# A two-block transformer kernel: compressed scores per projection in fp32, and scan products issued half a pair later with 17 factor buffers

## The chip, the cores and the metric

One core of one Trainium2 chip runs the whole program. The metric is the device time of one execution in microseconds (us).

## What is computed

Two blocks act on a sequence of 256 tokens of width 2048. The first is a sparse-attention block with a spatial gating branch. The second has an even layer (a bidirectional state-space scan next to a wide convolution) and an odd layer (neighbourhood attention). Two small parts matter here. In the first block each query is scored against 15 compressed keys:

```python
sc = jnp.einsum('bqgrd,bngd->bgrqn', qb, kc).astype(jnp.float32) * scale
sc = jnp.where(vc_mask, sc - slopes[:, :, None, None] * dc.astype(jnp.float32), NEG)
p_c = jax.nn.softmax(sc, axis=-1) * vc_mask
```

In the even layer the scan is, for each head and direction, a product of a decay matrix and a score matrix with the inputs:

```python
seg = A_cs[:, :, :, None] - A_cs[:, :, None, :]
Lmat = jnp.exp(jnp.where(tri, seg, -jnp.inf))
CB = jnp.einsum("bclgn,bcsgn->bclsg", Cc, Bc)
Y_diag = jnp.einsum("bclgsr,bcsgrp->bclgrp", CB[..., None] * Lmat, X)
```

## The kernel before

Nearly all work is projections. A weight piece of 128x1024 fp32 (`raw`) comes in by SP's DMA queue. ACT rounds it to `wh` (L98), DVE makes the rest `wl` (L99), and PE multiplies each of the eight 128x128 chunks three times (`mm3`, L120 to L122: high by high, high by low, low by high). A projection of the layers below is two such pieces, 48 matmuls. `raw`, `wh` and `wl` have four buffers each, so a new `wl` can only be written when PE is through with the piece four before. The output of a projection is a PSUM tile `acc`; while `K.wide` is set there are four of them.

The program is written as one stream, and a scheduler fixes the order of each engine's queue beforehand; each engine then runs its queue strictly in that order and waits at semaphores.

**Compressed scores (first block).** The compressed keys are split into a high and a low part, `kcbd[0]` and `kcbd[1]`. Eight query projections (`pj(0.125)`, evacuated by DVE at L321) are split into `qh` and `ql`. After all eight, 16 `mm3` of 32 columns each write the scores `scps`, and DVE starts the softmax (`sc`, L447).

**Scan (even layer).** There are 16 pairs of heads. For each pair, `ssd` makes nine factors `m`: `decay` takes a row of running sums from DRAM (`csb`, `cs0`), ACT does a Relu (L905) and an Exp (L906), and DVE multiplies by the scores (L907). The tag `m` has NM = 8 buffers. PE multiplies the first factor (L943) and then the other eight (L959) into `yps`, and DVE adds it to `yb` (L961). The pairs are spread over two runs of projections: 16 of `xs` (`conv5`: DVE makes four taps each, L876, on `cacc`; after each the transposes `xtp`), and then 16 of z (`za`: ACT Tanh L994, DVE L995). Behind z pair c is needed for `yb` times `za` (L1004). The sum of squares of all 16 closes the stage (`yss`, L210). After these come 16 projections `zb` (ACT Silu, L1043). Silu, and Exp with Tanh, are in different tables of ACT, so going from one to the other costs an ACT_TABLE_LOAD. All through these stages DVE also does the 480 taps of the wide convolution (`vb`, L845), metered out per weight piece.

**After `zb`.** The mean over `vb` (`lns`, `mean`, `lnm`) is taken, `yb` is split to `ah` and `al` (L164) for the output projection, and `vb` is centred (L1023).

Of the kernel before, what the change touches and what calls it, by code (L numbers as in the profile page):

```python
# [19 lines left out]
P = 128  # L20
# [15 lines left out]
NM, NK1 = 8, 6  # L36
# [217 lines left out]
def block1(K, a):  # L254
# [4 lines left out]
    with ExitStack() as ctx:  # L259
# [126 lines left out]
        kcbd = [wk.tile([P, 2, 2, 16], F32R, tag="kcbd%d" % i, bufs=1, name="kcbd%d" % i) for i in range(2)]  # L386
        for i in range(2):
            nc.vector.memset(kcbd[i].bitcast(F32), 0.0)
# [19 lines left out]
        for g in range(2):  # L408
            gs = slice(64 * g, 64 * g + 64)
            K.split(kcbd[0][gs, :, g, 0:15], kcbd[1][gs, :, g, 0:15],  # L410
                    cps[gs, :32].rearrange("q (p n) -> q p n", p=2)[:, :, 0:15])
            for p in range(2):
                nc.vector.tensor_copy(hidbd[gs, p, :, g, 0:15], hs[gs, 1, p, None, 0:15].to_broadcast([64, 4, 15]))
# [19 lines left out]
        qh, ql = t8("h0", F32R, "qh"), t8("h1", F32R, "ql")  # L433
        for j in range(8):
            K.split(qh[:, j, :], ql[:, j, :], pj(0.125))
# [3 lines left out]
        scps = K.ps.tile([P, 2, S], F32, tag="t", bufs=2, name="scps")  # L439
        for t in range(2):  # L440
            ts = slice(128 * t, 128 * t + 128)
            for j in range(8):
                p = j // 4
                K.mm3(scps[:, t, 32 * j : 32 * j + 32].rearrange("q (g n) -> q g n", g=2), qh[:, j, ts], ql[:, j, ts],
                      kcbd[0][:, p], kcbd[1][:, p], True, True)
# [235 lines left out]
def layer_e(K, a):  # L681
# [3 lines left out]
    with ExitStack() as ctx:  # L685
# [88 lines left out]

        def steps():
# [16 lines left out]
            yield 1.0  # L792
            nc.scalar.activation(ea[:64], par(K, "A_log")[:64], AF.Exp)
# [9 lines left out]
            for k, src in enumerate((dt, cs)):  # L803
                tp = K.ps.tile([P, 512], F32, tag="t", bufs=2, name="dtp")
                for i, (s0, s1) in enumerate(TT2[1:]):
                    nc.tensor.transpose(tp[:, 64 * i : 64 * i + 64], src[:, s0:s1], K.ident[:64, :64])
                for q in range(4):
                    r0 = 32 * (q // 2) + q % 2
                    nc.tensor.matmul(tp[32 * q : 32 * q + 32, 128:144], src[:, 0:32], K.ident[:64, r0 : r0 + 31 : 2],
                                     start=True, stop=True, skip_group_check=True)  # L810
                nc.scalar.activation(dtT[:, k].rearrange("p i r -> p (i r)"), tp[:, 0:128], AF.Copy)
                nc.scalar.activation(dt0[:, k], tp[:, 128:144], AF.Copy)
# [97 lines left out]
        def ssd(g):  # L910
# [19 lines left out]
            for i in (2 * g, 2 * g + 1):  # L930
                cs0 = wk.tile([P, T2], F32, tag="cs0", name="cs0")
                csbs = []
                for hh in range(2):
                    off = csd.offset + (2 * i + hh) * T2
                    csb = wk.tile([P, 2, T2], F32, tag="csb", bufs=3, name="csb")
                    nc.sync.dma_start(csb, bass.AP(tensor=csd.tensor, offset=off, ap=[[0, P], [32 * T2, 2], [1, T2]]))
                    csbs.append(csb)
                    for d in range(2):
                        q = 32 * (2 * d + hh)
                        nc.sync.dma_start(cs0[q : q + 32, :], bass.AP(tensor=csd.tensor, offset=off + 32 * d * T2, ap=[[0, 32], [1, T2]]))  # L940
                m0 = decay(cs0, dt0[:, 1, i : i + 1], dt0[:, 0, i : i + 1], cb0)
                yps = K.ps.tile([P, 512], F32, tag="o", bufs=1, name="yps")[:, :T2]
                nc.tensor.matmul(yps, xt[:, i, 0, :], m0, start=True, stop=False, skip_group_check=True)  # L943

                prods = []
                for d in range(2):
                    for ti in (1, 2):
                        s0, s1 = TT2[ti]
                        lo, hi = (s0, T2) if d == 0 else (0, s1)
                        for hh in range(2):  # L950
                            row = 32 * d + 2 * i + hh
                            m = decay(csbs[hh][:, d, lo:hi], dtT[:, 1, ti - 1, row : row + 1], dtT[:, 0, ti - 1, row : row + 1], C[d][ti])
                            prods.append((yps[64 * hh : 64 * hh + 64, lo:hi], xt[:, i, ti, 64 * hh : 64 * hh + 64], m))
                    if d:

                        prev = None
                        for k, (o, w, m) in enumerate(prods[::-1]):
                            with tc.issue_after(prev) if prev else nullcontext():
                                prev = nc.tensor.matmul(o, w, m, start=False, stop=k >= 6, skip_group_check=True).ins  # L959
                    yield 1.0  # L960
                nc.vector.tensor_tensor(yb[:, i, :], yb[:, i, :], yps, op=ALU.add)  # L961
                done[0] = i + 1
# [3 lines left out]
        def pump_ssd(n, upto=0):  # L966
            while ssdq and (n > 0 or done[0] < upto):
                try:
                    n -= next(ssdq[0])
                except StopIteration:  # L970
                    ssdq.pop(0)

# [422 lines left out]
```

## Time and profile before

| | us |
|---|---|
| median of 3 runs | 2270.6 (2270.43 to 2271.83) |
| the profiled execution | 2271.78 |
| its span, first to last instruction | 2269.9 |
| PE busy | 2218.4 (98%) |
| DVE busy | 1639.2 (72%) |
| ACT busy | 1162.1 (51%) |

The profiled execution is 1.2 us above the median, and 1.9 us of it lie outside the span. PE is busy for all but some 50 us, so the table says where to look: at the places where PE stands still, and at those where its clock is below full.

### The profile page before, as it was taken

Reading aid. Unit: us, or ns where it says so; the run is one execution under the profiler, and the core shown is the slowest. Engines: PE = TensorE matmul, PEld = TensorE weight load, DVE = VectorE, ACT = ScalarE, POOL = GpSimd, SP = SyncE. Lnnn points to the kernel's source line nnn. Section 1 sums busy time; section 2 is a strip of 40 time slices with the busy share of each in tenths; the row PEclk is TensorE's granted clock in tenths of the full one; section 3 lists DMA queues with packets and bytes.
Section 4 is the critical chain, followed back from the end, with each engine's and each line's share of the span. In section 5 each row is a group of like instructions: output and inputs, shape, how many; then the busy total and the mean of one; then the engine's idle time right before and its main releaser. Section 6 shows DMA issues by size and latency. Waiting matters only on the chain.

```text
span 2269.9 us, 44011 instructions
## 1 busy us (share of the span) xinstructions
PE 2218.4 (98%) x17702; PEld 2156.0 (95%) x17702; DVE 1639.2 (72%) x2891; ACT 1162.1 (51%) x2039; POOL 121.3 (5%) x114
## 2 busy tenths in 40 slices
PE   8999999999999999999998998899999999999997
PEld 7998799999999998999998998899999999999997
DVE  6557777555555669999999888798776666666654
ACT  4446654444444444454557887645444545444453
POOL 0000000000000230000000010002011000000011
PEclk9999999999999999999999999999999999999999
DMA  7642455555556554564454556354655555545453
GB/s 279 217 148 94 138 190 184 187 184 187 186 195 209 186 171 148 199 220 174 174 177 151 175 176 181 123 177 151 202 176 189 172 172 173 171 166 171 160 172 121
DMA packets 126412, 398.71 MB, mean 176 GB/s; under 512 B 16832, under 2 KB 33664, under 8 KB 125696
## 3 DMA queue, kind: packets, MB, share of 16 engines
q1 hardware_dynamic: 126064, 395.89, 51.6%
q8 instruction: 139, 2.28, 0.4%
q14 instruction: 65, 0.53, 0.1%
q10 hardware_dynamic: 144, 0.01, 0.0%
HBM read 391.45 MB, written 4.40 MB: 174 GB/s over the span
## 4 chain that ended last, share of the span: by engine, by line
PE 93%; DVE 3%; ACT 2%; DMA 1%; issue 1%; POOL 0%; SPq 0%; DVEq 0%; ACTq 0%; POOLq 0%
PE acc L120 28%; PE acc L122 28%; PE acc L121 28%; PE acc L156 1%; DVE wl L99 1%; DMA rawf<-in_w_in_fm 1%; PE yps L959 1%; DVE vb L845 1%; ACT wh L98 1%; PE o_ps L1210 1%; PE pt_ps L506 0%; PE sp L120 0%; PE sp L122 0%; PE sp L121 0%; PE o_ps L1208 0%
## 5 line engine op out<-in xcount | busy, mean ns | idle before, releaser
L98 ACT ACTIVATE wh<-raw 128x1024 fp32r<-128x1024 f32 x674 | 713.1, 1059 | 955.1 <-PE acc L121 580.1
L99 DVE TENSOR_TENSOR wl<-raw,wh 128x1024 fp32r<-128x1024 f32 x674 | 828.1, 1230 | 404.4 <-ACT wh L98 399.4
L120 PE MATMUL acc<-uh,wh 128*128 128x272 f32 (+1 forms) x1488 | 436.3, 293 | 15.7 <-DVE za L995 8.2
L121 PE MATMUL acc<-ul,wh 128*128 128x272 f32 (+1 forms) x1488 | 434.3, 292 | 0.0
L122 PE MATMUL acc<-uh,wl 128*128 128x272 f32 (+1 forms) x1488 | 434.3, 292 | 0.0
L120 PE MATMUL acc<-xh,wh 128*128 128x256 f32 (+1 forms) x1136 | 322.3, 284 | 0.0
L121 PE MATMUL acc<-xl,wh 128*128 128x256 f32 (+1 forms) x1136 | 322.3, 284 | 0.0
L122 PE MATMUL acc<-xh,wl 128*128 128x256 f32 (+1 forms) x1136 | 321.1, 283 | 0.1
L120 PEld LDWEIGHTS acc<-uh,wh 128*128 128x128 f32 (+1 forms) x1488 | 280.8, 189 | 19.5 <-DVE za L995 8.9
L122 PE MATMUL acc<-ouh,wl 128*128 128x256 f32 (+1 forms) x1024 | 296.6, 290 | 0.0
L121 PE MATMUL acc<-oul,wh 128*128 128x256 f32 (+1 forms) x1024 | 294.6, 288 | 0.0
L120 PE MATMUL acc<-ouh,wh 128*128 128x256 f32 (+1 forms) x1024 | 293.8, 287 | 0.0
L121 PEld LDWEIGHTS acc<-ul,wh 128*128 128x128 f32 (+1 forms) x1488 | 280.6, 189 | 3.5 <-issue 2.3
L122 PEld LDWEIGHTS acc<-uh,wl 128*128 128x128 f32 (+1 forms) x1488 | 280.2, 188 | 3.2 <-issue 2.3
L120 PEld LDWEIGHTS acc<-xh,wh 128*128 128x128 f32 (+1 forms) x1136 | 213.8, 188 | 1.4 <-DVE pj L319 0.4
L122 PEld LDWEIGHTS acc<-xh,wl 128*128 128x128 f32 (+1 forms) x1136 | 214.4, 189 | 0.4 <-DVE wl L99 0.3
L121 PEld LDWEIGHTS acc<-xl,wh 128*128 128x128 f32 (+1 forms) x1136 | 213.6, 188 | 0.5 <-issue 0.2
L122 PEld LDWEIGHTS acc<-ouh,wl 128*128 128x128 f32 x1024 | 192.5, 188 | 2.6 <-issue 2.6
L120 PEld LDWEIGHTS acc<-ouh,wh 128*128 128x128 f32 x1024 | 192.9, 188 | 0.0
L121 PEld LDWEIGHTS acc<-oul,wh 128*128 128x128 f32 x1024 | 192.7, 188 | 0.0
L845 DVE SCALAR_TENSOR_TENSOR vb<-early,par,vb 128x257 f32<-128x257 f32 (+9 forms) x330 | 150.3, 500 | 1.1 <-ACT vb L829 0.7
L204 POOL TENSOR_TENSOR sq<-sq 128x272 f32<-128x272 f32 (+1 forms) x44 | 50.6, 1150 | 741.0 <-issue 450.3
(417 smaller groups left out, 4295.7 us busy)
## 6 DMA issues: line engine op xcount, KB each, us to landing
raw<-in_e_w_in SPq DMA_DIRECT2D x184, 512.0 KB, 3.6
raw<-in_w_in_fm SPq DMA_DIRECT2D x140, 512.0 KB, 3.6
raw<-in_o_w_in SPq DMA_DIRECT2D x128, 512.0 KB, 3.9
raw<-in_e_w_out SPq DMA_DIRECT2D x64, 512.0 KB, 4.5
raw<-in_w_up SPq DMA_DIRECT2D x32, 512.0 KB, 3.6
raw<-in_w_out SPq DMA_DIRECT2D x32, 512.0 KB, 4.4
raw<-in_w_pg SPq DMA_DIRECT2D x32, 512.0 KB, 4.2
raw<-in_o_w_out SPq DMA_DIRECT2D x32, 512.0 KB, 4.4
```

The source lines that it names most:

```text
L98: nc.scalar.activation(wh, raw, AF.Copy)
L99: ins = nc.vector.tensor_tensor(wl, raw, wh.bitcast(F32), op=ALU.subtract)
L120: mm(out, lh, rh, start=start, stop=False)
L121: mm(out, lh, rl, start=False, stop=False)
L122: mm(out, ll, rh, start=False, stop=stop)
L156: self.nc.tensor.matmul(a, raws[c // 8][:, c % 8, :], x(c), start=c == 0, stop=c == 15)
L204: self.nc.gpsimd.tensor_tensor(acc, acc, sq, op=ALU.add)
L845: ins = nc.vector.scalar_tensor_tensor(v[:, lo:hi], u[:, lo + o : hi + o], par(K, "e_dw_w", 31 * b + k), v[:, lo:hi], op0=ALU.mult, op1=AL ...
L959: prev = nc.tensor.matmul(o, w, m, start=False, stop=k >= 6, skip_group_check=True).ins
L1210: nc.tensor.matmul(o_ps[64 * g : 64 * g + 64, ts], vt[:, 2 * t, 64 * g : 64 * g + 64], pt[:, g, :], start=False, stop=True, skip_group_che ...
```

## The change

There are four edits. The compressed keys stay in fp32 (one `kcbd`, written by ACT), and the scores of a query projection are two fp32 matmuls, issued right after that projection. The products of a scan pair are gathered in `finish` and issued after the first five factors of the next pair (or when the stage needs them), all nine in one run. The factors have 17 buffers; the memory for it comes from a smaller scratch area for dynamic DMA. Last, the transposes of `dt` come out before those of `cs` (`turned`).

```diff
-NM, NK1 = 8, 6
+NM, NK1 = 17, 6
...
-        kcbd = [wk.tile([P, 2, 2, 16], F32R, tag="kcbd%d" % i, bufs=1, name="kcbd%d" % i) for i in range(2)]
-        for i in range(2):
-            nc.vector.memset(kcbd[i].bitcast(F32), 0.0)
+        kcbd = wk.tile([P, 2, 2, 16], F32, tag="kcbd", bufs=1, name="kcbd")
+        nc.vector.memset(kcbd, 0.0)
...
-            K.split(kcbd[0][gs, :, g, 0:15], kcbd[1][gs, :, g, 0:15],
-                    cps[gs, :32].rearrange("q (p n) -> q p n", p=2)[:, :, 0:15])
+            nc.scalar.activation(kcbd[gs, :, g, 0:15], cps[gs, :32].rearrange("q (p n) -> q p n", p=2)[:, :, 0:15], AF.Copy)
...
+        scps = K.ps.tile([P, 2, S], F32, tag="t", bufs=2, name="scps")
         for j in range(8):
-            K.split(qh[:, j, :], ql[:, j, :], pj(0.125))
+            q = pj(0.125)
+            K.split(qh[:, j, :], ql[:, j, :], q)
+            for t in range(2):
+                nc.tensor.matmul(scps[:, t, 32 * j : 32 * j + 32].rearrange("q (g n) -> q g n", g=2),
+                                 q[:, 128 * t : 128 * t + 128], kcbd[:, j // 4], start=True, stop=True)
...
-        for t in range(2):
-            ts = slice(128 * t, 128 * t + 128)
-            for j in range(8):
-                p = j // 4
-                K.mm3(scps[:, t, 32 * j : 32 * j + 32].rearrange("q (g n) -> q g n", g=2), qh[:, j, ts], ql[:, j, ts],
-                      kcbd[0][:, p], kcbd[1][:, p], True, True)
...
-                m0 = decay(cs0, dt0[:, 1, i : i + 1], dt0[:, 0, i : i + 1], cb0)
-                yps = K.ps.tile([P, 512], F32, tag="o", bufs=1, name="yps")[:, :T2]
-                nc.tensor.matmul(yps, xt[:, i, 0, :], m0, start=True, stop=False, skip_group_check=True)
-
-                prods = []
+                prods = [decay(cs0, dt0[:, 1, i : i + 1], dt0[:, 0, i : i + 1], cb0)]
...
-                            prods.append((yps[64 * hh : 64 * hh + 64, lo:hi], xt[:, i, ti, 64 * hh : 64 * hh + 64], m))
-                    if d:
-
-                        prev = None
-                        for k, (o, w, m) in enumerate(prods[::-1]):
-                            with tc.issue_after(prev) if prev else nullcontext():
-                                prev = nc.tensor.matmul(o, w, m, start=False, stop=k >= 6, skip_group_check=True).ins
+                            prods.append((lo, hi, ti, hh, m))
+                    if d == 0:
+
+                        finish()
                     yield 1.0
-                nc.vector.tensor_tensor(yb[:, i, :], yb[:, i, :], yps, op=ALU.add)
-                done[0] = i + 1
+                ready.append((i, prods))
+
+        ready = []
+
+        def finish():
+
+
+            if not ready:
+                return
+            i, prods = ready.pop(0)
+            yps = K.ps.tile([P, 512], F32, tag="o", bufs=1, name="yps")[:, :T2]
+            prev = nc.tensor.matmul(yps, xt[:, i, 0, :], prods[0], start=True, stop=False, skip_group_check=True).ins
+            for k, (lo, hi, ti, hh, m) in enumerate(prods[:0:-1]):
+                with tc.issue_after(prev):
+                    prev = nc.tensor.matmul(yps[64 * hh : 64 * hh + 64, lo:hi], xt[:, i, ti, 64 * hh : 64 * hh + 64], m, start=False,
+                                            stop=k >= 6, skip_group_check=True).ins
+            nc.vector.tensor_tensor(yb[:, i, :], yb[:, i, :], yps, op=ALU.add)
+            done[0] = i + 1
...
+            if done[0] < upto:
+                finish()
...
-    nc = bacc.Bacc("TRN2", target_bir_lowering=False, num_devices=1)
+    nc = bacc.Bacc("TRN2", target_bir_lowering=False, num_devices=1, dynamic_dma_scratch_size=4096)
```

The scheduler's order of the two programs is the same on PE, ACT and DVE for most of the program. Three of the places that differ are shown here.

PE at the compressed scores, before: the 48 matmuls come in one run (31 of them, 22 of a projection in between, then the rest).

```order
L120 MATMUL acc<-xh,wh 128x256
L121 MATMUL acc<-xl,wh 128x256
L122 MATMUL acc<-xh,wl 128x256
L120 MATMUL scps<-kcbd_598,qh 128x32
L121 MATMUL scps<-kcbd_599,qh 128x32
L122 MATMUL scps<-kcbd_598,ql 128x32
L120 MATMUL scps<-kcbd_598,qh 128x32
L121 MATMUL scps<-kcbd_599,qh 128x32
```

The same engine after the change, at the first of the eight places:

```order
L120 MATMUL acc<-xh,wh 128x256
L121 MATMUL acc<-xl,wh 128x256
L122 MATMUL acc<-xh,wl 128x256
L438 MATMUL scps<-kcbd,pj 128x32 x2
L120 MATMUL acc<-xh,wh 128x256
L121 MATMUL acc<-xl,wh 128x256
```

Two fp32 matmuls now stand at eight places, 48 projection matmuls apart, half a projection behind the one whose queries they read.

ACT near the end of the scan, before: Silu of the first `zb` projections stands among the Exp of the last pairs, with a table load each way.

```order
L906 ACTIVATE m<-m 128x144
L1043 ACT_TABLE_LOAD
L1043 ACTIVATE zb<-acc 128x272
L906 ACT_TABLE_LOAD
L906 ACTIVATE m<-m 128x144
L201 ACTIVATE sq<-yb 128x272
L994 ACTIVATE zt<-acc 128x272
L905 ACTIVATE m<-csb,dtT 128x272
```

ACT at the same first `zb`, after (L908 is the Exp, L1007 the Tanh, L1056 the Silu):

```order
L908 ACTIVATE m<-m 128x272
L98 ACTIVATE wh<-raw 128x1024
L201 ACTIVATE sq<-yb 128x272
L1007 ACTIVATE zt<-acc 128x272
L98 ACTIVATE wh<-raw 128x1024
L201 ACTIVATE sq<-yb 128x272
L1007 ACTIVATE zt<-acc 128x272
L98 ACTIVATE wh<-raw 128x1024
L201 ACTIVATE sq<-yb 128x272
L98 ACTIVATE wh<-raw 128x1024
L1056 ACT_TABLE_LOAD
L1056 ACTIVATE zb<-acc 128x272
```

All factors and all z projections are now done before the first Silu; ACT's queue holds 5 table loads in place of 13.

DVE behind the mean over `vb`, before: `al` (L164) and the centring of `vb` (L1023) alternate, and the next weight piece comes after both.

```order
L1017 TENSOR_SCALAR mean<-lns 128x3
L218 TENSOR_SCALAR diag<-ident,mean 128x128 x2
L99 TENSOR_TENSOR wl<-raw,wh 128x1024
L164 TENSOR_TENSOR al<-yb,ah 128x272
L218 TENSOR_SCALAR diag<-ident,mean 128x128
L164 TENSOR_TENSOR al<-yb,ah 128x272 x7
L1023 TENSOR_TENSOR vb<-vb,lnm 128x272 x3
L164 TENSOR_TENSOR al<-yb,ah 128x272
L1023 TENSOR_TENSOR vb<-vb,lnm 128x272 x3
L164 TENSOR_TENSOR al<-yb,ah 128x272
L1023 TENSOR_TENSOR vb<-vb,lnm 128x272 x3
L164 TENSOR_TENSOR al<-yb,ah 128x272 x6
```

DVE at the same mean, after (L1030 the mean, L1036 the centring):

```order
L1030 TENSOR_SCALAR mean<-lns 128x3
L164 TENSOR_TENSOR al<-yb,ah 128x272 x3
L218 TENSOR_SCALAR diag<-ident,mean 128x128 x2
L164 TENSOR_TENSOR al<-yb,ah 128x272 x13
L218 TENSOR_SCALAR diag<-ident,mean 128x128
L99 TENSOR_TENSOR wl<-raw,wh 128x1024
L1073 TENSOR_TENSOR h_18187<-acc,hr 128x16
L1075 TENSOR_TENSOR h_18187<-acc,hr 128x4x32 x2
L1036 TENSOR_TENSOR vb<-vb,lnm 128x272 x12
```

All 16 `al` now stand together, and the weight piece comes before the centring.

## Rows read from the trace of the kernel before

**Rows 1.** The page: busy time and share of each engine.
```profile
PE 2218.4 (98%) x17702; PEld 2156.0 (95%) x17702; DVE 1639.2 (72%) x2891; ACT 1162.1 (51%) x2039; POOL 121.3 (5%) x114
```
**Rows 2.** Windows: stretch, width, then busy us of PE, PEld, DVE, ACT, POOL; PE clock, DMA.
```profile
1200.00:1250.00 50.00, 42.29 (x337) 40.22 (x336) 46.96 (x99) 40.06 (x103) 1.61 (x2) 1.00 0.47 151
1400.00:1450.00 50.00, 37.95 (x270) 34.22 (x269) 37.26 (x78) 36.34 (x79) 5.25 (x5) 0.90 0.38 118
```
**Rows 3.** Waits of PE from 1190 to 1470: us in total, times, longest.
```profile
PE acc L120 <- DVE za L995: 8.2, 2, 6.3
PE yps L959 <- DVE m L907: 5.0, 2, 3.2
PE acc L120 <- DVE cacc L876: 4.7, 3, 2.0
PE acc L120 <- ACT zb L1043: 2.8, 1, 2.8
PE yps L943 <- DVE m L907: 1.0, 2, 0.6
PE yss L210 <- POOL sq L204: 0.8, 1, 0.8
```
**Rows 4.** Windows around the compressed scores, columns as in rows 2.
```profile
144.00:148.00 4.00, 4.00 (x24) 4.00 (x23) 0.00 (x0) 0.00 (x0) 0.00 (x0) 0.57 0.37 131
148.00:152.00 4.00, 4.00 (x34) 4.00 (x34) 1.29 (x2) 1.06 (x1) 0.00 (x0) 0.91 0.01 4
152.00:156.00 4.00, 4.00 (x25) 4.00 (x25) 2.35 (x5) 0.70 (x1) 0.00 (x0) 0.66 0.33 123
```
**Rows 5.** Timeline of PE at scores and single fp32 matmuls: start us, us, instruction.
```profile
83.25 0.28 PE L120 MATMUL acc<-xh,wh 128*128 128x256 f32 x1
83.37 0.30 PE L407 MATMUL cps<-chs,w 128*128 128x32 f32 x2
...
83.71 0.28 PE L122 MATMUL acc<-xh,wl 128*128 128x256 f32 x1
...
148.03 0.26 PE L122 MATMUL scps<-kcbd,ql 128*128 128x32 f32 x1
...
150.37 0.26 PE L122 MATMUL scps<-kcbd,ql 128*128 128x32 f32 x1
...
1466.60 0.83 PE L210 MATMUL yss<-ones,sq 128*128 128x1 f32 x6 [0.76 <-POOL sq L204]
```
**Rows 6.** Timeline of ACT in the scan, with idle time before and its releaser.
```profile
1218.25 0.52 ACT L905 ACTIVATE m<-cs,dt 128x272 f32<-128x272 f32 x1 [2.59 <-PE yps L959]
...
1416.39 1.28 ACT L1043 ACT_TABLE_LOAD   x1
...
1418.10 1.28 ACT L906 ACT_TABLE_LOAD   x1
```
**Rows 7.** Windows of 6 us at the slow clock and at the mean, columns as in rows 2.
```profile
1422.00:1428.00 6.00, 6.00 (x43) 5.29 (x43) 1.67 (x3) 2.35 (x5) 0.00 (x0) 0.80 0.14 41
...
1434.00:1440.00 6.00, 5.68 (x33) 5.69 (x34) 2.65 (x7) 3.96 (x7) 0.81 (x1) 0.72 0.27 90
...
1542.00:1548.00 6.00, 3.32 (x16) 3.10 (x15) 6.00 (x14) 3.68 (x8) 4.03 (x5) 0.66 0.35 107
1548.00:1554.00 6.00, 6.00 (x40) 6.00 (x39) 4.17 (x6) 1.94 (x4) 4.54 (x3) 0.77 0.84 265
```
**Rows 8.** Waits of PE over the whole span, the three at the mean.
```profile
PE acc L122 <- DVE wl L99: 2.7, 1, 2.7
...
PE lnm L219 <- DVE diag L218: 0.7, 1, 0.7
PE acc L121 <- DVE al L164: 0.7, 1, 0.7
```
**Rows 9.** Waits of SP's queue from 1190 to 1470, and a landing time.
```profile
SPq L936 <- ACT m L905: 32.1, 12, 4.3
...
raw<-in_e_w_in SPq DMA_DIRECT2D x184, 512.0 KB, 3.6
```

More of the change, by code (lines that the diff above doesn't have):

```diff
@@ L433, in block1 @@
         qh, ql = t8("h0", F32R, "qh"), t8("h1", F32R, "ql")
+        scps = K.ps.tile([P, 2, S], F32, tag="t", bufs=2, name="scps")
         for j in range(8):
-            K.split(qh[:, j, :], ql[:, j, :], pj(0.125))
-        ptc = wk.tile([P, 2, S], F32, tag="ptc", bufs=1, name="ptc")
-        scps = K.ps.tile([P, 2, S], F32, tag="t", bufs=2, name="scps")
-        for t in range(2):
-            ts = slice(128 * t, 128 * t + 128)
-            for j in range(8):
-                p = j // 4
-                K.mm3(scps[:, t, 32 * j : 32 * j + 32].rearrange("q (g n) -> q g n", g=2), qh[:, j, ts], ql[:, j, ts],
-                      kcbd[0][:, p], kcbd[1][:, p], True, True)
+            q = pj(0.125)
[3 more added lines that the diff above has]
+                                 q[:, 128 * t : 128 * t + 128], kcbd[:, j // 4], start=True, stop=True)
+        ptc = wk.tile([P, 2, S], F32, tag="ptc", bufs=1, name="ptc")
         sc = wk.tile([P, 2, 16, 16], F32, tag="sc", bufs=1, name="sc")
@@ L773, in layer_e, with turned @@
         dt0 = wk.tile([P, 2, 16], F32, tag="dt0", bufs=1, name="dt0")
+        def turned(k, src):
+            tp = K.ps.tile([P, 512], F32, tag="t", bufs=2, name="dtp")
+            for i, (s0, s1) in enumerate(TT2[1:]):
+                nc.tensor.transpose(tp[:, 64 * i : 64 * i + 64], src[:, s0:s1], K.ident[:64, :64])
+            for q in range(4):
+                r0 = 32 * (q // 2) + q % 2
+                nc.tensor.matmul(tp[32 * q : 32 * q + 32, 128:144], src[:, 0:32], K.ident[:64, r0 : r0 + 31 : 2],
+                                 start=True, stop=True, skip_group_check=True)
+            nc.scalar.activation(dtT[:, k].rearrange("p i r -> p (i r)"), tp[:, 0:128], AF.Copy)
+            nc.scalar.activation(dt0[:, k], tp[:, 128:144], AF.Copy)
         def steps():
@@ L792, in steps @@
             yield 1.0
+            turned(0, dt)
+            yield 1.0
             nc.scalar.activation(ea[:64], par(K, "A_log")[:64], AF.Exp)
@@ L802, in steps @@
             nc.sync.dma_start(csd, cs)
[L803 to L812, printed above, removed]
+            turned(1, cs)
             yield 1.0
```

## The prediction, made before the changed kernel had run

> **What bounds the kernel now.** I read the page first. PE is busy for 98% of the span [rows 1], so a change can only gain where PE stands still, where its clock is below full, or where it is given less to do. The windows of 50 us come next, to find such places. The reader is to see that in 1200 to 1250 PE has 42.29 us of work in 50 while DVE has 46.96, and that in 1400 to 1450 nobody is full: PE 37.95, DVE 37.26, ACT 36.34 [rows 2]. The first place is short of DVE time. The second is a chain in which the engines take turns.
>
> The waits of PE name these chains. From 1190 to 1470, which is the scan, PE waits 22.5 us in six groups [rows 3]: 5.0 and 1.0 for a factor `m`, 4.7 for the taps of `conv5`, 8.2 for `za`, 2.8 for `zb`, 0.8 before the closing sum. `za`, `zb` and `cacc` are evacuations: PE wants their PSUM tile back. The timeline of ACT says why they are late. ACT waits 2.59 us for PE's products before it may start the next pair's factors, since eight buffers hold less than one pair of nine [rows 6]. Near 1416 a Silu among the Exp costs it two table loads of 1.28 us each, and `za` stands behind them. So PE waits for ACT, which waits for PE.
>
> Last, the clock. In the three windows of 4 us behind the first run of scores it is 0.57, 0.91 and 0.66 of full [rows 4]: PE did narrow matmuls of 32 columns, and then went between the levels of 2.4 and 1.2 GHz while it did wide ones. The same shows after the stalls of the scan (0.80, 0.72) and near the mean over `vb` (0.66, 0.77) [rows 7].
>
> **The change, part by part.**
>
> *Scores.* Removed are 48 matmuls. From 148.03 to 150.37 stand 21 starts in a row, 2.34 us, so 0.111 us each [rows 5]: 5.4 us of a PE that has no slack there. With them goes their clock loss, as far as the narrow run caused it: 4 x (0.43 + 0.09 + 0.34) = 3.4 us [rows 4]. Added are 16 fp32 matmuls of the same shape as `cps`. That one stands between two projection matmuls whose starts are 83.25 and 83.71 with one more between; without it they would be 2 x 0.12 apart, so it costs 0.22 us. Three in a row with one column take 0.83, or 0.28 each [rows 5]. They come in twos, so I take 0.24, nearer to the same shape: 3.8 us, between 3.5 and 4.5. Two such matmuls between 48 wide ones resemble `cps` more than a run of 31, so I count the clock as recovered; if it is not, the bound is 1.6 us. The sum is 5.4 + 3.4 - 3.8 = 5.0 us gained, between 0.9 and 5.3.
>
> The row gives one fp32 matmul as two records and 0.22 us. The Trainium skill (FP8 and Floating Point Precision, TensorE Precision Notes) says that true fp32 makes four passes through the array. By that the 16 would be 64 passes against 48 before; at 0.111 us each they would take 7.1 us, the scores would gain 1.7, and the forecast would be 2246. I go by the row, which is of the very shape.
>
> The new wait is that of the scores for their `pj`. Half a projection lies between, 24 matmuls of 0.12, 2.9 us, which covers one DVE evacuation; without it all of PE's queue would stand behind it eight times. `scps` holds one of two PSUM tiles of its tag through eight projections; in PE's order no other tile of that tag is written in between, so I count nothing.
>
> *Scan.* With 17 buffers the nine factors of a pair and five of the next (14) can be alive together, so ACT no longer waits for PE, and PE issues its nine products when they have long been made. At stake are the 22.5 us of rows 3 and the clock behind the stalls, 6.00 x 0.20 + 5.68 x 0.28 = 2.8 us [rows 7]: 25.3 in all. What stays is counted in the order. DVE can be at most four `wl` pieces ahead of PE, as there are four buffers. For each evacuation I count how many pieces ahead of the point where PE needs the tile DVE's queue has `wl` standing before it. Four means no lead is left. Before, that count is four for x projections 3, 4 and 14 and z projections 13 to 15, which are the places of the waits for `cacc`, `za` and `zb`. After, it is four for x 3 and x 11, three for four others, and two at most for every z. For the last factor of a pair it was three for pairs 0, 1 and 13; now no pair has more than two. So the 12.8 us around `za`, `zb`, `m` late in the scan and the closing sum should go, and the 5.0 for the other factors too. But the 4.7 for `cacc` are DVE's own load, which the change does not lessen [rows 2]. With x 11 new, I leave 5.5 us there, and 2.0 for the denser end: the 16 pairs now stand within 1294 projection matmuls, before 1525. Kept 7.5, gained 17.8; the bounds are 0 and 25.3.
>
> The eight table loads that go (10.2 us of ACT) are inside these waits and not counted again. The early factors that ACT now makes before `conv5`, and `dt` transposed early, I put at nothing: ACT is busy for 51% [rows 1]; without that cover it is the nine Relu and nine Exp of a pair, some 5 us, once. The smaller scratch area I put at nothing as well, as the DMAs that wait or are waited for here are SP's; were they slower, 3.6 us to landing [rows 9] would grow.
>
> *The mean over `vb`.* PE waits 2.7, 0.7 and 0.7 us there, 4.1 [rows 8], and loses 3.32 x 0.34 + 6.00 x 0.23 = 2.5 to the clock [rows 7]. The `wl` it waits for stood behind all `al` and 15 centrings, while POOL worked beside DVE. After, the 16 `al` and one `diag` are all that is ahead of it. I take 5.0 of 6.6; bounds 0 and 6.6.
>
> *Sum.* 5.0 + 17.8 + 5.0 = 27.8. The profiled execution took 2271.8, so 2244.0; it is 1.2 above the median of the runs, so 2242.8, or 2243. All upper bounds together give 2233.
>
> **The rivals.**
>
> *DVE stays the bound.* The waits for `m` and `za` turn into waits for `cacc` and `wl`, because DVE has as much to do in a scan that is a sixth shorter. For it: DVE at 46.96 of 50 while PE waits [rows 2]. Against it: in 1400 to 1450 DVE has 12.7 us free. Price: half of the 25.3 stays (12.7 in place of 7.5) and the mean gains nothing: 2243 + 5.2 + 5.0, some 2253.
>
> *The buffers do nothing.* The stalls come back under other names, and only the scores gain, with the clock or without: 2266 to 2270. For it: PE still runs strictly in order. Against it: the counts above, and that the table loads are gone from the queue.
>
> *SP's queue, on the other side.* Each pair loads two `csb` and four `cs0`, and a `csb` load waits until a Relu frees one of three buffers; weight pieces stand behind it. SP waits 32.1 us for that already [rows 9]. In the new order only two weight pieces stand between the loads of one pair and the next in the late scan, before four. If each of the last eight pairs made one weight piece late by 3.5 us, the 27.8 would be gone; at the longest wait and a landing, 4.3 + 3.6 = 7.9, each, it would be 63 us: 2243 + 63 = 2306. Against it: with SP waiting that long, no wait of ACT for a weight piece is in the list from 1190 to 1470, and in both orders a weight load behind a `csb` is for a piece four or five ahead of ACT.
>
> **How the numbers follow.** The forecast has 0.69 (2235 to 2249), DVE as the bound 0.22 (2249 to 2262), buffers without effect 0.04, SP 0.05. The likeliest is 2243. The range is 2235 to 2257: down to most of the upper bounds, up through the middle of the first rival, with 0.09 and part of DVE's case beyond. About 0.2%, 4.5 us, is what a measurement can tell from no change; the first two cases are faster than that, the third is the same, the last slower: 0.91, 0.04, 0.05.
>
> **What would show it.** The scores: no clock below 1 between 140 and 156, and 16 matmuls of 0.22 to 0.28. The scan: no wait of ACT's L907 for `yps`, one table load at its end, waits of PE for `za` near zero, some for `cacc` left near 1205 to 1225. The mean: no wait of PE for `wl`. It would be wrong if PE's idle time between 1190 and 1460 were above 12 us, if the clock still fell behind the scores, or if ACT waited for `raw`.

## The result, and the profile after

The changed kernel takes 2254.2 us, the median of 4 runs (2251.3 to 2254.8); the kernel before took 2270.5 beside it (4 runs, 2264.6 to 2271.8). The ratio is 0.9926, with a 95% interval from 0.9913 to 0.9939: some 16 us faster, where 27.8 were forecast. The profiled execution took 2254.3, of which 2252.4 lie in the span.

The page shows the smaller part of it. PE is busy for 7 us less, and still for 98% of the span; ACT has the eight table loads less (compare [rows 1]).

```profile
PE 2211.5 (98%) x17686; PEld 2147.9 (95%) x17686; DVE 1636.2 (73%) x2888; ACT 1150.6 (51%) x2031; POOL 124.5 (6%) x114
```

Where the time came from is read best from landmarks that both kernels have. These are the rows of four groups of instructions before the change (the times are the first and the last start in us): the first split `qh` ahead of the scores, the first `cacc` of `conv5`, the last `zb`, the first matmul of `lnv`.

```profile
L163 ACT ACTIVATE qh<-pj x8: 398/400/402, 102.4 to 142.2; 128x256 fp32r<-128x256 f32 x8
...
L872 ACT ACTIVATE cacc<-acc,par x32: 555/562/588, 1069.0 to 1298.4; 128x272 f32<-128x272 f32 x32
...
L1043 ACT ACTIVATE zb<-acc x16: 374/378/399, 1417.7 to 1527.5; 128x272 f32<-128x272 f32 x16
...
L210 PE MATMUL lnv<-ones,sq x6: 165/250/250, 1565.4 to 1565.9; 128*128 128x1 f32 x6
```

The same four after the change:

```profile
L163 ACT ACTIVATE qh<-pj x8: 398/400/402, 102.0 to 144.9; 128x256 fp32r<-128x256 f32 x8
...
L874 ACT ACTIVATE cacc<-acc,par x32: 559/562/591, 1064.4 to 1302.8; 128x272 f32<-128x272 f32 x32
...
L1056 ACT ACTIVATE zb<-acc x16: 377/378/398, 1425.3 to 1515.4; 128x272 f32<-128x272 f32 x16
...
L210 PE MATMUL lnv<-ones,sq x6: 165/250/250, 1547.9 to 1548.3; 128*128 128x1 f32 x6
```

From the first `qh` to the first `cacc` it was 966.6 us and is now 962.4: the scores gained 4.2. From there to the last `zb` it was 458.5 and is 451.0: the scan gained 7.5. From the last `zb` to `lnv` it was 37.9 and is 32.5: the mean over `vb` gained 5.4. That is 17.1 of the 17.5 between the spans; 0.4 lie ahead of `qh`, and behind `lnv` both kernels take the same. So two of the three terms of the sum came near their forecast (5.0 and 5.0), and the scan, for which 17.8 stood there, lacks ten. Each of these parts is read from one execution on either side. In a second profile of the changed kernel (s7 below) the scores gained 4.2 again, the scan 9.5 and the mean 3.9, so the last two are good to some 2 us.

What PE still waits for in the scan, from 1190 to 1470 (us in total, times, longest; compare [rows 3]):

```profile
PE acc L120 <- DVE cacc L878: 6.3, 3, 3.2
PE yps L970 <- DVE m L909: 3.6, 1, 3.6
PE xtp L994 <- ACT four L900: 3.1, 1, 3.1
PE acc L120 <- DVE za L1008: 1.4, 1, 1.4
```

The waits for `zb` and `yss` are gone, that for `za` went from 8.2 to 1.4. But `cacc` grew from 4.7 to 6.3, the wait for `m` is still 3.6, and a wait of 3.1 for `four` is new. These are 14.4 us in all. ACT's waits before a Relu in the same stretch include these two:

```profile
ACT m L907 <- PE yps L970: 6.3, 4, 3.6
...
ACT m L907 <- DMA csb<-csd: 2.1, 1, 2.1
```

So ACT still waits for PE's products (9.7 for them before the change), and once for a `csb` row, which it did not before. The windows say where PE's waits are (stretch, width, then busy us of PE, PEld, DVE, ACT, POOL; PE clock, DMA):

```profile
1192.00:1204.00 12.00, 8.45 (x64) 7.63 (x64) 12.00 (x32) 6.77 (x16) 0.00 (x0) 0.90 0.41 137
1204.00:1216.00 12.00, 9.64 (x75) 7.76 (x71) 11.61 (x24) 10.14 (x28) 1.69 (x2) 0.95 0.26 80
...
1252.00:1264.00 12.00, 12.00 (x98) 11.07 (x97) 5.59 (x9) 10.61 (x32) 0.00 (x0) 1.00 0.58 170
1264.00:1276.00 12.00, 5.67 (x35) 5.05 (x34) 8.00 (x13) 9.52 (x26) 0.00 (x0) 0.75 0.62 198
1276.00:1288.00 12.00, 12.00 (x76) 11.68 (x76) 9.38 (x22) 7.11 (x18) 0.00 (x0) 0.83 0.14 50
1400.00:1450.00 50.00, 50.00 (x404) 48.43 (x403) 48.78 (x99) 25.64 (x45) 7.40 (x7) 1.00 0.47 161
```

The late stretch, 37.95 of 50 before [rows 2], is full at a clock of 1.00. The first place, 1192 to 1216, is about as it was, and PE's clock is now below 1 there. And in 1264 to 1276 stands a stall that the kernel before did not have: PE works 5.67 of 12 us at a clock of 0.75, and 0.83 in the next. This time it isn't DVE that is full, as it was at the first place (12.00 and 11.61 of 12): DVE was busy for only 5.59 and 8.00, while ACT was for 10.61 and 9.52.

PE's timeline has the two waits of the new stall (start, length, instruction, and the idle time before it with its releaser):

```profile
1270.08 0.47 PE L994 MATMUL xtp<-ident,four 128*128 128x128 f32 x1 [3.14 <-ACT four L900]
...
1274.17 0.59 PE L120 MATMUL acc<-uh,wh 128*128 128x272 f32 x1 [3.19 <-DVE cacc L878]
```

And this is ACT just before. Between the weight pieces that start at 1250.62 and 1261.60 lie 11 us. Most of them are Relu and Exp for two pairs of heads; 1.39 are idle, and there the chain of work has a `csb` load of 3.80 us (from 1257.81). The second pair goes on around the next three pieces:

```profile
1250.62 1.06 ACT L98 ACTIVATE wh<-raw 128x1024 fp32r<-128x1024 f32 x1 [1.95 <-PE acc L121]
...
1252.00 2.09 ACT L907 ACTIVATE m<-csb,dtT 128x256 f32<-128x256 f32 x6
...
1255.05 1.85 ACT L908 ACTIVATE m<-m 128x256 f32<-128x256 f32 x7
...
1260.60 1.09 ACT L907 ACTIVATE m<-csb,dtT 128x256 f32<-128x256 f32 x3 [1.39 <-PE acc L122]
1261.60 1.05 ACT L98 ACTIVATE wh<-raw 128x1024 fp32r<-128x1024 f32 x1
1262.55 1.12 ACT L907 ACTIVATE m<-csb,dtT 128x144 f32<-128x144 f32 x3
1263.57 1.35 ACT L908 ACTIVATE m<-m 128x272 f32<-128x272 f32 x4
1264.83 0.41 ACT L884 ACTIVATE ct<-cacc 128x272 f32<-128x272 f32 x1
...
1265.35 1.04 ACT L98 ACTIVATE wh<-raw 128x1024 fp32r<-128x1024 f32 x1
...
1267.15 0.85 ACT L908 ACTIVATE m<-m 128x144 f32<-128x144 f32 x3
1267.90 1.05 ACT L98 ACTIVATE wh<-raw 128x1024 fp32r<-128x1024 f32 x1
...
1269.72 0.31 ACT L900 ACTIVATE four<-xs 128x128 f32<-128x128 f32 x1
```

`four`, for which PE waits at 1270.08, is the last of these rows. It needs `xs`, which needs `ct` (1264.83) and the taps; `ct` and `four` stand in ACT's queue behind or between the factors. With eight buffers ACT could not do this: it had to stop for PE's products between two pairs, as in [rows 6]. At this place before the change:

```profile
1266.65 1.06 ACT L98 ACTIVATE wh<-raw 128x1024 fp32r<-128x1024 f32 x1 [0.83 <-PE acc L121]
...
1269.88 0.52 ACT L905 ACTIVATE m<-cs,dt 128x272 f32<-128x272 f32 x1 [1.38 <-PE yps L959]
...
1274.46 1.04 ACT L98 ACTIVATE wh<-raw 128x1024 fp32r<-128x1024 f32 x1
```

The longest stretch without a weight piece there was the 7.8 us between these two. With 17 buffers ACT need not stop between the pairs.

For the other runs below, the loss of PE in a place is added up from windows of 2 us: 2 less the busy time is its waits, and the busy time by one less the clock is what the clock cost. For the kernel before this gives 7.7 us of waits at the first place (1180 to 1252), 1.9 at the second (1252 to 1330), and 12.1 of waits with 3.4 of clock at the late one (1330 to 1450). After, it is 6.6 and 1.3 of clock, then 7.7 and 3.5, then nothing.

The scores are as forecast in their parts, too. Around one of the eight places PE's timeline shows two fp32 matmuls as four records:

```profile
109.75 0.28 PE L122 MATMUL acc<-xh,wl 128*128 128x256 f32 x1
109.86 0.53 PE L438 MATMUL scps<-kcbd,pj 128*128 128x32 f32 x4
110.23 0.36 PE L120 MATMUL acc<-xh,wh 128*128 128x256 f32 x1
...
110.55 0.28 PE L122 MATMUL acc<-xh,wl 128*128 128x256 f32 x1
```

From 109.75 to 110.55 it is 0.80 us for what takes 3 x 0.12 without them, so 0.44 for two, 0.22 each: the lower of the two prices in [rows 5]. And the clock does not fall behind them (compare [rows 4]):

```profile
148.00:152.00 4.00, 4.00 (x36) 4.00 (x35) 3.94 (x8) 1.89 (x3) 0.00 (x0) 1.00 0.59 217
152.00:156.00 4.00, 4.00 (x30) 3.74 (x29) 3.81 (x8) 2.40 (x8) 0.00 (x0) 1.00 0.38 135
```

At the mean the wait for `wl` is gone. PE still waits 1.4 us from 1500 to 1570, the most for these two (compare [rows 8]):

```profile
PE lns L210 <- POOL vsum L854: 0.6, 1, 0.6
PE acc L121 <- DVE al L164: 0.6, 1, 0.6
```

### The profile page after: what moved, and what is told of

The parts are those of the page before. It is cut to its first block, busy times and chain, and to the rows that moved or that the text cites. A ratio compares the mean times of both kernels' runs of the same rounds, so it can differ in the third digit from the quotient of the medians.

```text
span 2252.4 us, 43952 instructions
## 1 busy us (share of the span) xinstructions
PE 2211.5 (98%) x17686; PEld 2147.9 (95%) x17686; DVE 1636.2 (73%) x2888; ACT 1150.6 (51%) x2031; POOL 124.5 (6%) x114
## 4 chain that ended last, share of the span: by engine, by line
PE 94%; DMA 2%; DVE 2%; ACT 1%; issue 0%; SPq 0%; POOL 0%; DVEq 0%; ACTq 0%; POOLq 0%
PE acc L120 29%; PE acc L122 29%; PE acc L121 29%; PE acc L156 1%; PE yps L970 1%; DMA rawf<-in_w_in_fm 1%; DMA csb<-csd 1%; PE o_ps L509 1%; ACT m L907 1%; PE pt_ps L503 1%; PE o_ps L1223 1%; PE sp L120 1%; PE sp L122 0%; PE sp L121 0%; DVE wl L99 0%; PE o_ps L1221 0%
## 5 line engine op out<-in xcount | busy, mean ns | idle before, releaser
L204 POOL TENSOR_TENSOR sq<-sq 128x272 f32<-128x272 f32 (+1 forms) x44 | 57.4, 1305 | 704.9 <-ACT sq L201 703.9
```

The costliest lines, as they stand in the source:

```text
L204: self.nc.gpsimd.tensor_tensor(acc, acc, sq, op=ALU.add)
```

## The experiments

The question was where the ten microseconds of the scan went. The theory: with 17 buffers ACT makes the factors of two pairs back to back, and weight pieces and evacuations stand behind them ("twos"). Rivals: `csb` rows that come late, DVE without time for `cacc`, and the order of PE's products. Beside them, two of the four edits were run alone (the scores; the buffers with the smaller scratch area), and the gathered products were taken out of the whole. The early transposes of `dt` and the scratch area were not tried apart. Each kernel ran five rounds beside the kernel before; "scan" is the time from the first `cacc` to the last `zb`, and the loss columns are waits + clock.

| kernel | median us | ratio to before, 95% | scan us | first place | second place | late |
|---|---|---|---|---|---|---|
| before | 2270.2 to 2272.3 | 1 | 458.5 | 7.7 + 0 | 1.9 + 0 | 12.1 + 3.4 |
| changed | 2254.2 | 0.9926 (0.9913 to 0.9939) | 451.0 | 6.6 + 1.3 | 7.7 + 3.5 | 0 |
| changed, again (s7) | 2254.4 | 0.9926 (0.9910 to 0.9943) | 449.0 | 6.6 + 1.3 | 7.1 + 1.9 | 0 |
| scores only (s1) | 2268.4 | 0.9984 (0.9975 to 0.9994) | 461.6 | 6.5 + 2.7 | 1.9 + 0 | 11.7 + 6.0 |
| 17 buffers only (s2) | 2254.1 | 0.9926 (0.9913 to 0.9939) | 445.0 | 5.1 + 2.8 | 3.8 + 1.4 | 0 |
| 14 buffers (s3) | 2254.7 | 0.9924 (0.9911 to 0.9937) | 447.8 | 6.7 + 3.1 | 4.5 + 1.7 | 0 |
| four csb (s4) | 2251.9 | 0.9915 (0.9903 to 0.9928) | 446.9 | 6.6 + 1.3 | 5.2 + 2.1 | 0 |
| products back (s5) | 2252.4 | 0.9917 (0.9899 to 0.9934) | 444.7 | 4.7 + 2.8 | 3.9 + 1.3 | 0 |
| scores back (s6) | 2255.9 | 0.9929 (0.9911 to 0.9946) | 447.0 | 5.1 + 2.9 | 5.2 + 2.5 | 0 |
| fewer taps (s8) | 2256.5 | 0.9931 (0.9913 to 0.9949) | 447.5 | 6.6 + 1.8 | 5.2 + 1.9 | 0 |
| taps later (s9) | 2258.3 | 0.9945 (0.9929 to 0.9961) | 446.8 | 4.8 + 2.7 | 5.3 + 3.0 | 0 |
| start later (s10) | 2253.4 | 0.9925 (0.9910 to 0.9939) | 450.7 | 8.3 + 1.7 | 5.6 + 2.8 | 0 |
| products back, 12 buffers (s11) | 2252.4 | 0.9919 (0.9903 to 0.9935) | 446.1 | 5.4 + 3.3 | 4.2 + 0 | 0.2 + 0 |
| Relu on POOL (s12) | 2264.6 | 0.9968 (0.9957 to 0.9979) | 459.9 | 6.8 + 1.3 | 2.8 + 1.7 | 11.0 + 1.7 |

Runs of one kernel differ by some 2 to 12 us, so medians two apart are not told apart here. The waits are steadier than the clock: the changed kernel, profiled twice, has 15.7 and 15.0 us of waits in 1180 to 1520 (within 0.5 was expected) with the same clock loss at the first place, but 3.5 and 1.9 at the second. The 1.9 at the second place stands at x projection 14 in the kernel before (and in s1), not at 11, where the changed kernel has its stall:

```profile
1295.73 0.39 PE L120 MATMUL acc<-uh,wh 128*128 128x272 f32 x1 [1.94 <-DVE cacc L876]
```

One more caution: with each edit the scheduler may order the queues anew, also where the edit has nothing to do. So a difference of some 2 us between two edited kernels at one place need not be the edit's own.

**s1, the scores alone.** The kernel before with the hunks of `kcbd` and `scps`.

```diff
-            K.split(qh[:, j, :], ql[:, j, :], pj(0.125))
+            q = pj(0.125)
+            K.split(qh[:, j, :], ql[:, j, :], q)
+            for t in range(2):
+                nc.tensor.matmul(scps[:, t, ...], q[:, 128 * t : 128 * t + 128], kcbd[:, j // 4], start=True, stop=True)
...
```

> The kernel before with the compressed-score edit alone. Both theories: the first cbps of the scan comes 4.6 us earlier, as in the changed kernel (1190.9 to 1186.3), no clock below 1 between 130 and 156, and the scan and the mean are as before: 2270.5 - 4.6 = 2266, between 2265 and 2267. If the scores gain nothing by themselves: 2270.

From `qh` to `cacc` it takes 962.4, the same 4.2 less as in the changed kernel, and the clock is 1.00 from 100 to 200. The whole gains 3.1 at the median, less than the 4.6 expected, but its interval (1.4 to 5.7 us) holds both 4.6 and 4.2. In the one profile the scan took 3.1 more: its waits were 1.6 less, but the clock cost 2.7 at the first place, where before there was no loss, and 2.6 more at the late one. So the term shows where it arises. Whether the scan really gives part of it back is not shown, since the clock differs as much between two profiles of one program.

**s2, the buffers alone.** The kernel before with two numbers changed.

```diff
-NM, NK1 = 8, 6
+NM, NK1 = 17, 6
...
-    nc = bacc.Bacc("TRN2", target_bir_lowering=False, num_devices=1)
+    nc = bacc.Bacc("TRN2", target_bir_lowering=False, num_devices=1, dynamic_dma_scratch_size=4096)
```

> The kernel before with 17 factor buffers and the smaller scratch area alone: products where they were, scores and transposes as before. Theory 'twos' (17 buffers let ACT make the factors of two pairs back to back, with weight pieces and evacuations behind them): the late waits for za and zb go, a new stall of PE of 5 to 7 us near x projections 8 to 11 comes, and the sum is that of the changed kernel without its 4.6 of the scores: 2256 to 2261. Rival 'the later products do it': PE issues products whose factors are late, the late waits stay, 2266 to 2271.

These two lines gain 17.4 us, all that the whole change does, without the scores; that is 2 us below the 2256 to 2261 expected. The scan takes 13.5 less, and the stretch from `zb` to `lnv` 33.1 in place of 37.9, so the gain at the mean comes with the buffers as well. The rival (the later products do it) falls. The second stall is there, as "twos" said, but with 3.8 + 1.4 it is half as large as in the changed kernel.

**s3, 14 buffers,** and **s4, four `csb` buffers.** The changed kernel with one number each.

```diff
-NM, NK1 = 17, 6
+NM, NK1 = 14, 6
```

> The changed kernel with 14 factor buffers in place of 17, the least that the gathered products need. Theory 'twos': ACT's queue spreads the factors, so the two waits of PE between 1260 and 1280 (3.1 for four, 3.2 for cacc) and the half clock behind them (3.4) mostly go, the late scan stays free of waits: 2245 to 2250. Rival 'csb loads' (ACT waits for csb rows that come late with three buffers): no change there, 2252 to 2256. Rival 'DVE': the waits come back for cacc or wl elsewhere, 2252 to 2258; if 14 buffers bring the waits of ACT for yps back, 2258 to 2268.

```diff
-                    csb = wk.tile([P, 2, T2], F32, tag="csb", bufs=3, name="csb")
+                    csb = wk.tile([P, 2, T2], F32, tag="csb", bufs=4, name="csb")
```

> The changed kernel with four csb buffers in place of three. Rival 'csb loads': the 3.8 and 2.6 us for csb in the chain of work and most of the 9.7 us at 1260 to 1280 go, 2245 to 2250. Theory 'twos': ACT's queue still has two pairs back to back there, the wait for four and cacc stays above 4 us, 2251 to 2256.

Neither settles it alone. With 14 buffers the loss at the second place falls from 11.2 (or 9.0 in the second profile) to 6.2, less than "twos" asked for, and the 2245 to 2250 did not come. The stall did not go, it moved: 3.39 for `cacc` end at 1287.45, at x projection 13. With four `csb` the waits there are 5.2 in place of 7.7 and 7.1: the wait for `za` (1.4, which the chain of work of the changed kernel leads back to a `csb` row) is gone, that for `four` is 1.6 in place of 3.1 and 2.1, that for `cacc` stays (3.5). But s6 and s8 below keep three `csb` buffers and have the same 5.2, with the same two waits, so the 2 us can't be put down to the fourth buffer. The 2245 to 2250 of the rival `csb` did not come either. Both medians lie within the runs of the changed kernel (2251.3 to 2257.9).

**s5 to s7, what the gathered products do.** In s5 the products stand where they stood before the change; s6 is the changed kernel with the scores of before; s7 is the changed kernel once more.

```diff
-                prods = [decay(cs0, dt0[:, 1, i : i + 1], dt0[:, 0, i : i + 1], cb0)]
+                m0 = decay(cs0, dt0[:, 1, i : i + 1], dt0[:, 0, i : i + 1], cb0)
+                yps = K.ps.tile([P, 512], F32, tag="o", bufs=1, name="yps")[:, :T2]
+                nc.tensor.matmul(yps, xt[:, i, 0, :], m0, start=True, stop=False, skip_group_check=True)
...
-                    if d == 0:
-                        finish()
+                    if d:
+                        prev = None
+                        for k, (o, w, m) in enumerate(prods[::-1]):
+                            with tc.issue_after(prev) if prev else nullcontext():
+                                prev = nc.tensor.matmul(o, w, m, start=False, stop=k >= 6, skip_group_check=True).ins
...
```

> The changed kernel with the products put back where they were before (one with the first factor, eight behind the last); scores, 17 buffers and the early transposes of dt stay. Theory 'buffers alone' (the 17 buffers give the gain, the gathered products take some of it back): the scan loses as little as with 17 buffers alone (10.3 us of waits and 4.1 of clock), the scores add their 4.2: 2248 to 2252. Rival 'the gains don't add' (what one edit gains before the scan, the scan gives back): 2253 to 2256, as the changed kernel.

> The changed kernel with the compressed scores of before. Theory 'buffers alone': PE's waits in the scan are those of the changed kernel (6.6, 6.3 and 1.4 at its three places), the scores' 4.2 are missing: 2256 to 2260. Rival 'the gains don't add': 2252 to 2255, with waits as small as with 17 buffers alone.

> The changed kernel once more, as the measure for the other runs here: 2251 to 2256, PE's waits in the scan within 0.5 us of 15.7, its clock losses free to differ.

Without the gathered products PE waits 8.6 us at the two places in place of 13.7 to 14.3, and the scan takes 444.7 in place of 451.0 and 449.0. PE's waits of s5 from 1190 to 1470 are three:

```profile
PE acc L120 <- DVE cacc L878: 4.7, 3, 3.5
PE yps L961 <- DVE m L909: 3.5, 1, 3.5
PE xtp L983 <- ACT four L900: 0.4, 1, 0.4
```

So the gathered products gained nothing here; in these profiles they cost 4 to 6 us of the scan, and 2 between s2 and s6. At the medians it is 2 us, which these runs don't tell from nothing. s5's waits are those of "buffers alone" (10.6 in 1180 to 1520), its median of 2252.4 is just above the 2248 to 2252. s6 (2255.9) falls between the two forecasts, 2252 to 2255 and 2256 to 2260, and so do its waits: 5.1 and 5.2 where "buffers alone" had 6.6 and 6.3. With 17 buffers the scores bring 1.7 us at the medians (s6 to changed; s2 to s5, there with the early transposes), where they bring 4.2 between `qh` and `cacc`. The runs can't say whether that is a loss or noise, so it stays open whether the gains add.

The second stall is made of two waits that go different ways. That for `four` follows ACT's run without a weight piece: 3.1 and 2.1 after 11.0 and 9.9 us (the changed kernel twice), 1.6 after 8.5 to 10.5 (s4, s6, s8), 0.3 to 0.4 after 6.3 (s2, s5, where a weight piece stands in the middle). That for `cacc` does not: it is 3.2 to 3.5 in all of these, with the products gathered or not. The kernel before has neither at this place.

**s8 and s9, DVE's load at the first place.** Two ways to take taps from it.

```diff
-        taps.extend((b, us[b], k) for k in range(31) if k != 15 for b in bs)
+        taps.extend((b, us[b], k) for k in range(31) if k != 15 and not (k < 5 and bs[-1] in (8, 10)) for b in bs)
```

> The changed kernel with 20 of the 480 taps of the wide convolution left out (the first five of blocks 7 to 10; vb is not that of the reference), some 8 us of DVE that stand before the first scan stall. Theory 'DVE's load sets the first stall': PE's waits between 1180 and 1228 fall from 6.6 to below 2.5, the rest stays: 2245 to 2250. Rival 'the 18 factors of the first two pairs set it' (DVE has to multiply them all when their cb comes): the wait for m (3.6) stays, 2251 to 2256.

```diff
-TAPS = [20, 1, 0, 1, 4]
+TAPS = [20, 0.5, 0, 1, 4]
```

> The changed kernel with half as many taps per weight piece during the 16 projections before the scan; the 32 taps that this leaves are done later, with those of the z and zb projections. Of the 37 taps between 1180 and 1228 most should be gone from that stretch. Theory 'DVE's load sets the first stall': PE's waits there fall from 6.6 to below 2.5 and the total to 2246 to 2251. Rival 'the order sets it' (PE's products of the first pair stand too early in its queue, and DVE has 18 factors to multiply when the first cb comes): 5 us or more of waits stay, 2252 to 2256.

s8 did not test DVE's load: the taps are handed out by number per weight piece, so those left out were missing at the end, and 38 still stood between 1180 and 1228 (37 in the changed kernel). It shows something else: at the second place, where it has nearly the same work in another order, it waits 5.2 us against 7.7 and 7.1. s9 did lighten the first place: 25 taps stand there between 1180 and 1228 (11, 6, 8 and none in windows of 12 us), and PE's waits up to 1250 are 3.5 for `m` and 1.2 for `cacc`. The part for `cacc` fell from 3.1 to 1.2, that for `m` stayed. So both theories hold a part: DVE's load makes the wait for `cacc`, and taking load away does not touch the 3.5 for `m`; the order theory puts them down to where PE's first products stand. The total of neither came (2258.3). In the profile, itself the slowest of six runs (2262.2), the taps came due at the mean: PE waits 6.5 us there for DVE (`h`, L1075), and from `zb` to `lnv` it takes 44.8.

**s10, a later start.** The tasks of the scan are handed out from x projection 4 on.

```diff
-            pump_ssd(RATE[0])
+            if i > 3:
+                pump_ssd(RATE[0])
```

> The changed kernel with the scan's tasks handed out from x projection 4 on, three projections later; all else as it was. Theory 'the order sets the first stall': the wait for m (3.5) goes, since the first products stand behind two more projections, and with the cacc waits the first place falls below 2.5; 2247 to 2251. Theory 'DVE's load': the waits only change their name to cacc, 5 us or more stay. The later start packs the rest tighter, so the second place (5.2 to 6.3) may keep its size or grow by up to 2.

The wait for `m` goes, as the order theory said, and comes back as `cacc`:

```profile
PE acc L120 <- DVE cacc L878: 6.5, 3, 3.2
PE yps L967 <- DVE yb L972: 1.3, 1, 1.3
```

With 8.3 us of waits the first place is no better. DVE is full there (11.45 and 11.96 of 12 us from 1192 to 1216), so what the later start saves, the next wait takes: 5 us or more stay, as the theory of DVE's load had it. The second stall moved with the scan, from x projection 11 to 14:

```profile
1289.27 0.33 PE L994 MATMUL xtp<-ident,four 128*128 128x128 f32 x1 [1.76 <-ACT four L900]
...
1293.36 0.59 PE L120 MATMUL acc<-uh,wh 128*128 128x272 f32 x1 [3.54 <-DVE cacc L878]
```

**s11, 12 buffers with the products back,** and **s12, ACT's half of the work moved away.** Two tests of "twos" at the second place.

```diff
-NM, NK1 = 17, 6
+NM, NK1 = 12, 6
```

> The changed kernel with the products put back where they were and 12 factor buffers, so that ACT can't have two pairs of factors done at once. Theory 'twos': PE's waits between 1252 and 1330 fall from 3.9 to below 2 as in the kernel before (1.9), and the late scan stays free: 2246 to 2251. Rival 'fewer buffers bring the waits of ACT for yps back': the late scan (1396 to 1450) has waits again, 2255 to 2266.

```diff
-            nc.scalar.activation(m, csb, AF.Relu, scale=-1.0, bias=bias)
-            nc.scalar.activation(m, m, AF.Exp, scale=-1.0)
+            nc.gpsimd.tensor_scalar(m, csb, bias, None, op0=ALU.max)
+            nc.scalar.activation(m, m, AF.Exp, scale=-1.0, bias=bias)
...
-            nc.vector.tensor_scalar(la, dt, ea[:64], -1.0, op0=ALU.mult, op1=ALU.mult)
+            nc.vector.tensor_scalar(la, dt, ea[:64], 1.0, op0=ALU.mult, op1=ALU.mult)
```

> The changed kernel with the Relu of the 144 factors moved from ACT to POOL (as a maximum with the column's own sum; the sums are kept with the other sign, so that Exp takes the bias). ACT has half the factor work in the scan, all else stays. Theory 'ACT's queue makes the second stall' (18 factors of two pairs stand before the weight pieces and evacuations of x projections 9 to 11): PE's waits between 1252 and 1330, 5.6 and 1.5 us with 1.9 to 3.5 of clock behind them, fall below 2.5 in all, and the total comes to 2243 to 2249. Rival 'DVE has no time for cacc there': 4 us or more of waits stay, 2251 to 2256. Third way: POOL's pieces are too slow (its additions of 272 columns take 0.8 to 1.3 us, ACT's Relu 0.3 to 0.5) and PE waits for m: 2256 to 2270.

With 12 buffers the late scan is as good as free, so the waits that eight buffers caused there need no 17; the second place loses 4.2 and no clock, against 3.9 + 1.3 with 17. That is not the fall below 2 that was expected. But the stall itself is gone: no wait for `four`, and from 1252 to 1300 a single one for `cacc`:

```profile
1277.65 0.39 PE L120 MATMUL acc<-uh,wh 128*128 128x272 f32 x1 [0.21 <-DVE cacc L878]
```

The rest of the 4.2 are other waits: 0.9 for `early`, 1.8 for `yb` and, at 1304.38, 1.3 for `cacc`. With the Relu on POOL the second place loses 2.8 + 1.7, where the changed kernel loses 7.7 + 3.5 or 7.1 + 1.9. PE's waits there are now:

```profile
1269.40 0.33 PE L994 MATMUL xtp<-ident,four 128*128 128x128 f32 x1 [0.34 <-ACT four L900]
...
1296.15 0.39 PE L120 MATMUL acc<-uh,wh 128*128 128x272 f32 x1 [2.49 <-DVE cacc L878]
```

These 4.5 in all are more than the 2.5 that "ACT's queue" allowed. But 2.49 of them stand at x projection 14, where the kernel before has its 1.94; of the stall at 11 only the 0.34 are left. ACT was the only engine whose work was made less. So the stall hangs on the factors of two pairs that ACT has in a row: it goes when the buffers can't hold two pairs (s11) or half of that work leaves ACT (s12), and it moves when the scan does (s10). That POOL's slower pieces also spread the factors in time can't be separated here. The total lost all the same (2256 to 2270 was the third way): later POOL is the bound. In 1350 to 1400 it is busy for 49.80 of 50 us, and PE for 42.75:

```profile
1350.00:1400.00 50.00, 42.75 (x324) 37.08 (x325) 43.40 (x89) 32.65 (x72) 49.80 (x51) 1.00 0.61 172
```

Most of its pieces take 1.01 us:

```profile
L907 POOL TENSOR_SCALAR m<-csb,dtT 128x256 f32<-128x256 f32 (+3 forms) x128 | 127.6, 1011 | 93.0 <-PE yps L967 89.1 <-DMA csb<-csd 3.7 <-PE cbps L924 0.2
```

No version is clearly faster than the changed kernel; s4, s5 and s11 have the lowest medians, 2 us below it.

## Why the prediction was right in direction and too large

**The sum.** The 2254.2 lies in the range (2235 to 2257), but not in the forecast's own part of it (2235 to 2249, which had 0.69). It lies where the rival with DVE as the bound was priced (2249 to 2262, 0.22), and that rival's mechanism did not come true either, as told below. So it is luck that the range holds the time. By the prediction's own signs its account of the scan is wrong: PE's idle time between 1190 and 1460 was to be 12 us at most and is 14.4, and ACT was not to wait for `yps` and does.

**Scores: right.** 5.0 forecast, 4.2 measured. The fp32 matmuls took 3.5 in all (8 x 0.44) where 3.8 stood, and the clock was recovered, as taken. So the removed run was worth 7.7 and not 5.4 + 3.4 = 8.8; where the 1.1 went is not shown. (Its 48 matmuls stand in the trace as 21, 2 and 25, with 11 of a projection after the first and after the second group.) The sentence on the four passes of true fp32 (the Trainium skill, FP8 and Floating Point Precision, TensorE Precision Notes) would have given 1.7 by the prediction's estimate; the trace, with 0.22 us for one of 32 columns, sides with the row.

**Mean: right.** 5.0 forecast, 5.4 and 3.9 measured, and as worked out: no wait for `wl`, and in the first profile a clock of 1.00 from 1540 on. s2 shows that it comes with the buffers.

**Scan: the late part right, the kept part too small.** The late waits went entirely, 12.1 and 3.4 of clock, and nothing came back from the denser end (2.0 had been left for it). The step that failed is "kept 7.5 = 5.5 around `cacc` + 2.0". In 1180 to 1520 the changed kernel keeps 15.7 of waits and 4.8 of clock, of which 1.4 belong to the mean: 19.1 in place of 7.5. It failed in two ways:

1. *The wait for `m` was to go, "and the 5.0 for the other factors too".* 3.6 stayed at the first place, and 3.3 or more in every kernel here but s10. The count was of weight pieces ahead in DVE's queue; but there DVE is full, and has to multiply the factors of two pairs as soon as the first `cb` is there. ACT still waits for `yps` as well, 6.3 us in four, 3.6 of them at 1203: the 17 factors that it makes early use up all the buffers. s10 shows that a later start of the scan only renames the wait.
2. *x projection 11 was named as the place with no lead, and given 0.8 (5.5 in place of 4.7).* The count saw DVE's queue alone. What was late there was ACT: 11 us without a weight piece, then `ct` and `four` behind factors. The windows show it (DVE busy for 5.59 of 12, ACT for 10.61), and s11 and s12, in which ACT can't have two pairs done at once or has half the work, have no such stall there. Of the size it had in the changed kernel, 11.2 or 9.0, 5.2 are there without the gathered products (s2, s5); these add the rest, 4 to 6 by s5, 2.5 by s2 and s6.

What would have shown it beforehand is in the order: 14 Relu and 8 Exp in ACT's queue with no weight piece between them. The prediction said "ACT no longer waits for PE" and took that for a gain; it did not ask what stands behind ACT's longer run.

The first rival came to 2253, nearly what was measured, but by another road: it let the mean gain nothing and made DVE the bound of the scan. The mean gained, and DVE bounds only the first place. SP's queue made no weight piece late: ACT has no wait for `raw` from 1190 to 1470, and SP's wait behind the Relu fell from 32.1 [rows 9] to 14.7. Its `csb` loads are now in the chain of work at the second place, but what they cost is not shown (s4).

**Left open:** through which of ACT's late pieces the wait for `cacc` comes about, as it stays 3.5 where the longest run without a weight piece is only 6.3 us (s2, s5); why the gathered products lengthen ACT's run at the second place, since they change PE's order and, through the scheduler, ACT's at once; and whether a scan without the stall at the first place can be had while DVE has its taps there.

## What to carry to other kernels

When buffers are added so that an engine need not wait, look at what stands behind its longer run, on its own queue: the wait that went may have been what let other work through. Count the lead of an evacuation on every engine that it passes, not on the one that was the bound before. And run the numbers of a change apart from its code: here two constants gave as much as the whole change.

## What was not expected of the hardware

The clock did not follow the length of the waits. At the first place the kernel before has 7.7 us of waits and no clock below 1; with the scores alone there are 6.5, and the window from 1204 to 1216 has 0.88:

```profile
1204.00:1216.00 12.00, 8.00 (x60) 7.26 (x61) 12.00 (x28) 8.07 (x24) 1.61 (x2) 0.88 0.47 137
```

The same program lost 3.5 and 1.9 us of clock at its second stall in two runs. So a gain or loss of 2 or 3 us that shows only as clock in one profile can't be put down to an edit.
